# Splitting half of the W1 weights by a casting and an accumulating DMA

## The chip, the cores and the metric

The kernel runs on one core of a Trainium2 chip. A core has a matrix engine (PE, with its weight loads listed apart as PEld), a vector engine (DVE), a scalar engine (ACT), GpSimd (POOL) and SyncE (SP), and 16 DMA engines that all DMA queues share. The metric is the device time of one execution in microseconds, as the median of the runs.

## The reference

The program is a two-layer decoder trunk over 256 tokens of width 2048 in float32. Layer 0 is a gated short convolution, layer 1 latent attention with 16 heads. Each is followed by a squared-ReLU MLP of hidden width 8192, and every sublayer ends in a layer norm of `alpha*x + f(x)`. What matters here is the MLP, which runs once in each layer:

```python
def sq_relu_mlp(x, w1, w2):            # x: 256x2048, w1: 2048x8192, w2: 8192x2048
    return jnp.square(jax.nn.relu(x @ w1)) @ w2
```

## The kernel before

**Precision by two parts.** PE multiplies in a reduced float32 format (float32r). Each float32 operand is therefore split into a high part (its value rounded to float32r) and a low part (the rest, again as float32r), and a product is the sum of high by high, high by low and low by high. For a weight the split is the function `split` (lines 109 to 112): ACT writes `hi` by a copy that rounds (line 111), and DVE writes `lo = raw - hi` (line 112).

**The stream of weight units.** All weights come from DRAM in units of 128 partitions by 1024 float32 values (512 KB), in the order in which PE will use them; this order is the list `stream` (lines 64 to 83). A unit is loaded by SP into one of 5 `raw` buffers (`load_raw`, lines 130 to 133) and split into one of 8 `hi` and one of 8 `lo` buffers (`RAW, WA = 5, 8`, line 33). A `hi` or `lo` buffer is free again when PE has done the last product with the unit eight places earlier. `take` (lines 171 to 183) hands PE the next units, and before that calls `prepare` (lines 135 to 165) for units up to `LOOK = 5` places further on.

**The MLP.** It runs in 8 passes (`NQ = 8`), each over 1024 hidden columns. A pass has three stages:

- *W1 stage*: 8 chunks of 128 hidden columns. A chunk takes two units, a first half (input rows 0 to 1023) and a second half (input rows 1024 to 2047). For each of 16 blocks, `mm_run` issues a product of 512 columns with the high weights (line 190) and one of 256 columns with the low weights (line 194). The result is added up (`whole`, lines 300 to 304), passed through ReLU and square on ACT (lines 562 and 563) and split (lines 308 and 309). In pass 0, the first one of each MLP, other products are used for this stage (`mm_wide`).
- *fast stage* (in 13 of the 16 passes of the two MLPs): half of the output columns by seven products in place of eight (`down_fast`, lines 287 to 298). Each of its 4 weight pairs takes two loads and three pairs of `hi` and `lo` buffers, and some DVE work of its own (lines 142 to 165).
- *down stage*: the remaining output columns with 4 units for each block of 512 columns (`down`, lines 259 to 269), so 8 units after a fast stage.

**What sets the order.** The order of the instructions on each engine and DMA queue is fixed before the run by the scheduler of the framework, which plans with estimated times: of what it holds to be ready it puts the earlier in the program first. So an instruction may stand on its engine well ahead of work that the program names before it. At run time every engine and every queue works strictly in the planned order; what waits for a semaphore holds up all that stands behind it. POOL has almost nothing to do before the change: a few memsets, and four DMAs (line 869) at the beginning of the last stage that load the final gain and offset vectors.

Of the kernel before, what the change touches and what calls it, by code (L numbers as in the profile page):

```python
# [9 lines left out]
F32 = mybir.dt.float32  # L10
F32R = mybir.dt.float32r
AF = mybir.ActivationFunctionType
ALU = mybir.AluOpType
# [9 lines left out]
QC = FF // NQ // P  # L23
# [22 lines left out]
def trunk(ctx: ExitStack, tc: tile.TileContext, xT, vecs, w_in, w_out, w_kv, w_q, w_uk, w_uv,  # L46
          w_qn, w_qp, w_o, w1, w2, w2f, cosT, sinT, mask, ident, gb, out):
    nc = tc.nc
# [10 lines left out]
    def halves(w):  # L59

        lead = len(w.shape) - 2
        return [(w,)] if lead == 0 else [h for i in range(w.shape[0]) for h in halves(w[i])]

    stream = []
# [1 line left out]
        stream += halves(w_in[NC + m]) + halves(w_in[2 * NC + m]) + halves(w_in[m])  # L66
    stream += halves(w_out)

    def mlp_stream(l):
        out = []  # L70
        for q in range(NQ):
            out += halves(w1[l, q * QC:(q + 1) * QC])
            lead = 0
            if q in FAST[l]:
                out += [(w2f[l, q, j, 0], w2f[l, q, j, 1]) for j in range(QC // 2)]
                lead = 2
            out += halves(w2[l, q, lead:])
        return out

    stream += mlp_stream(0) + halves(w_kv) + halves(w_q)  # L80
    for g in range(4):
        stream += halves(w_uk[g]) + halves(w_qn[g]) + halves(w_uv[g]) + halves(w_qp[g])
    stream += halves(w_o) + mlp_stream(1)

    class Banks:

# [20 lines left out]
    ready = {}  # L107

    def split(hi, lo, src):

        nc.scalar.copy(hi, src)  # L111
        nc.vector.tensor_tensor(lo, src, hi.bitcast(F32), ALU.subtract)  # L112

    def tiled(w):
        return w.rearrange("p (b c) -> p b c", c=P)

    def parts(i):
        return tuple(whl.tile([P, 8, P], F32R, tag=t, name=f"{t}{i}") for t in ("hi", "lo"))
# [11 lines left out]
    def load_raw(i, src):  # L130
        raw = raws.tile([P, 1024], F32, tag="raw", name=f"raw{i}")
        nc.sync.dma_start(raw, src)
        return raw

    def prepare(i):

        if len(stream[i]) == 1:
            raw = load_raw(i, stream[i][0])
            hi, lo = ready[i] = parts(i)
            split(hi, lo, tiled(raw))  # L140
            return
        r1, r2 = (load_raw(f"{i}_{j}", src) for j, src in enumerate(stream[i]))
        out = []

        def finished(r, name):
            hi, lo = parts(name)
            split(hi, lo, tiled(r))
            out.append((hi, lo))

        b22, (b21, b12) = r1[:, BW:], (r2[:, :BW], r2[:, BW:])  # L150
        finished(r1, f"{i}_1")
        t = raws.tile([P, 1024], F32, tag="raw", name=f"raw{i}_t")
        two = "p (a c) -> p a c"
        nc.vector.tensor_tensor(t.rearrange(two, a=2), b12.unsqueeze(1).to_broadcast([P, 2, BW]),
                                r1.rearrange(two, a=2), ALU.subtract)
        finished(t, f"{i}_t")
        nc.vector.tensor_tensor(b12, b22, t[:, :BW], ALU.subtract)
        finished(r2, f"{i}_2")
        t4 = r1[:, :BW]
        nc.vector.tensor_tensor(t4, b21, b12, ALU.subtract)  # L160
        f = state["fast"].tile([P, 2, BW], F32R, tag="t4", name=f"t4_{i}")
        split(f[:, 0, :], f[:, 1, :], t4)
        b1, t13, b2 = ([[v.rearrange("p b c -> p (b c)")[:, o:o + BW] for v in w] for o in (0, BW)] for w in out)
        ready[i] = {"11": b1[0], "22": b1[1], "21": b2[0], "T2": b2[1], "T1": t13[0], "T3": t13[1],
                    "T4": [f[:, 0, :], f[:, 1, :]]}
# [5 lines left out]
    def take(halves=2):  # L171

        i = state["next"]
        state["next"] += halves
        ahead = -sum(size(j) for j in range(i, i + halves))
        for j in range(i, len(stream)):
            ahead += size(j)
            if ahead > LOOK:
                break
            if j >= state["split"]:  # L180
                prepare(j)
                state["split"] = j + 1
        return [ready.pop(i + j) for j in range(halves)]
# [295 lines left out]
    for half, cuts in enumerate(FIRST):  # L479
        pieces = [load(2 * u + half, first[:, GROUP * half + u, :], cuts) for u in range(GROUP)]  # L480
        for b0, b1 in zip(cuts, cuts[1:]):
            at = slice(8 * half + b0, 8 * half + b1)
# [502 lines left out]
```

## Time and profile before

| what | value |
|---|---|
| median of 2 runs | 2053.64 us (2053.06 to 2054.22) |
| span of the profiled execution, first to last instruction | 2049.4 us |
| PE busy | 2030.6 us (99%) |
| DVE busy | 1662.8 us (81%) |
| ACT busy | 1194.1 us (58%) |
| POOL busy | 4.5 us |
| weight loads of SP's queue | 381.04 MB, 58.7% of 16 DMA engines' time |
| mean granted clock of PE | 0.997 |

The page of the profile gives the span of the profiled execution and no total beyond it; the median of the runs is 4.2 us above that span. In the rows of groups, the columns are line, engine, operation, what is written and read, shapes and count; then, after the bar, the total busy time and the mean of one in ns; then the idle time of the engine in front of them and what ended it. Matmuls overlap each other in these rows, so their means are longer than the pace at which they follow one another.

### The profile page before, as it was taken

What the parts mean: (1) busy time and instruction counts of PE and PEld (TensorE: products, weight loads), DVE (VectorE), ACT (ScalarE), POOL (GpSimd) and SP (SyncE); (2) the same over time, 40 slices, a digit from 0 to 9 for tenths busy, and PEclk for the clock granted to TensorE, in tenths of its full rate; (3) what the DMA queues carried; (4) which work ended last, traced back from release to release, by engine and by line L of the source; (5) the groups of instructions that cost most, each with busy time, mean ns of one, the idle gap of its engine ahead of it and who ended that gap; (6) DMA issues with size and microseconds to landing.
All of it is one profiled execution on the core that took longest, in us unless ns stands there. A gap on an engine that the chain in (4) does not pass through costs nothing.

```text
span 2049.4 us, 30194 instructions
## 1 busy us (share of the span) xinstructions
PE 2030.6 (99%) x11208; PEld 1760.4 (86%) x11208; DVE 1662.8 (81%) x2602; ACT 1194.1 (58%) x1860; POOL 4.5 (0%) x25
## 2 busy tenths in 40 slices
PE   9999999999999999999999999999999999999997
PEld 8888888988888888888889998898888888888885
DVE  7667677678898988989788878776879888898988
ACT  6444445676566565655656665566656656566562
POOL 0000000000000000000000000000000000000000
PEclk9999999999999999999999999999999999999998
DMA  8666666564746557465755544656475664756653
GB/s 308 202 188 187 186 185 194 159 211 136 249 142 223 193 167 250 143 226 173 234 169 164 166 124 142 197 174 196 138 236 161 196 218 156 243 153 217 212 165 137
DMA packets 108003, 385.32 MB, mean 188 GB/s; under 512 B 11984, under 2 KB 13392, under 8 KB 107856
## 3 DMA queue, kind: packets, MB, share of 16 engines
q1 hardware_dynamic: 107136, 381.04, 58.7%
q0 software_dynamic: 576, 2.10, 0.3%
q8 instruction: 88, 1.44, 0.3%
q14 instruction: 59, 0.48, 0.1%
q10 hardware_dynamic: 144, 0.26, 0.0%
HBM read 381.25 MB, written 2.10 MB: 187 GB/s over the span
## 4 chain that ended last, share of the span: by engine, by line
PE 97%; DVE 1%; DMA 1%; issue 0%; ACT 0%; SPq 0%; DVEq 0%
PE ps_u L190 34%; PE ps_u L194 17%; PE ps_d L248 7%; PE ps_d L247 7%; PE ps_d L249 7%; PE ps_f L249 4%; PE ps_f L248 4%; PE ps_f L247 4%; PE ps_w L224 1%; PE ps_w L222 1%; PE ps_w L223 1%; PE ps_g L222 1%; PE ps_g L224 1%; PE ps_g L223 1%; PE ps_wo L190 1%; PE S L788 1%
## 5 line engine op out<-in xcount | busy, mean ns | idle before, releaser
L112 DVE TENSOR_TENSOR lo<-raw,hi 128x1024 fp32r<-128x1024 f32 x712 | 861.7, 1221 | 299.0 <-ACT hi L111 294.3
L111 ACT CAST hi<-raw 128x1024 fp32r<-128x1024 f32 x712 | 742.2, 1049 | 526.6 <-PE ps_u L190 289.5
L190 PE MATMUL ps_u<-xhl,hi 128*128 128x512 f32 x1792 | 632.2, 398 | 0.0
L194 PE MATMUL ps_u<-xhl,lo 128*128 128x256 f32 x1792 | 503.0, 281 | 0.0
L190 PEld LDWEIGHTS ps_u<-xhl,hi 128*128 128x128 f32 x1792 | 336.5, 188 | 82.3
L194 PEld LDWEIGHTS ps_u<-xhl,lo 128*128 128x128 f32 x1792 | 338.5, 189 | 0.5
L190 PE MATMUL ps_u<-xhl_a,hi 128*128 128x512 f32 x720 | 253.4, 396 | 0.0
L248 PE MATMUL ps_d<-lo,h 128*128 128x512 f32 x608 | 236.9, 390 | 0.0
L249 PE MATMUL ps_d<-hi,h 128*128 128x512 f32 x608 | 236.8, 390 | 0.0
L247 PE MATMUL ps_d<-hi,h 128*128 128x512 f32 x608 | 236.6, 389 | 0.0
L194 PE MATMUL ps_u<-xhl_a,lo 128*128 128x256 f32 x720 | 202.9, 282 | 0.0
L190 PEld LDWEIGHTS ps_u<-xhl_a,hi 128*128 128x128 f32 x720 | 135.2, 188 | 31.9
L194 PEld LDWEIGHTS ps_u<-xhl_a,lo 128*128 128x128 f32 x720 | 135.8, 189 | 0.0
L248 PEld LDWEIGHTS ps_d<-lo,h 128*128 128x128 f32 x608 | 114.1, 188 | 24.2 <-DVE lo L112 0.4
L247 PEld LDWEIGHTS ps_d<-hi,h 128*128 128x128 f32 x608 | 114.2, 188 | 24.0
L249 PEld LDWEIGHTS ps_d<-hi,h 128*128 128x128 f32 x608 | 114.1, 188 | 23.9
L111 ACT CAST hi_t<-raw_t 128x1024 fp32r<-128x1024 f32 x52 | 54.8, 1054 | 77.8 <-PE ps_u L190 41.8
L190 PE MATMUL ps_u<-z,hi 128*128 128x512 f32 x256 | 89.0, 392 | 0.0
L562 ACT ACTIVATE fh<-fh 128x256 f32<-128x256 f32 x112 | 46.4, 414 | 72.0 <-DVE fh L304 72.0
L222 PE MATMUL ps_w<-xd,hi 128*128 128x258 f32 x256 | 72.5, 284 | 0.0
L224 PE MATMUL ps_w<-xd,hi 128*128 128x258 f32 x256 | 72.5, 285 | 0.0
L223 PE MATMUL ps_w<-xd,lo 128*128 128x258 f32 x256 | 72.3, 282 | 0.0
(235 smaller groups left out, 3254.8 us busy)
## 6 DMA issues: line engine op xcount, KB each, us to landing
raw<-in_w_dram SPq DMA_DIRECT2D x408, 512.0 KB, 4.4
raw<-in_w2f_dram SPq DMA_DIRECT2D x104, 512.0 KB, 3.6
raw<-in_w_in_dram SPq DMA_DIRECT2D x90, 512.0 KB, 4.2
raw<-in_w_out_dram SPq DMA_DIRECT2D x32, 512.0 KB, 3.6
raw<-in_w_o_dram SPq DMA_DIRECT2D x32, 512.0 KB, 3.9
raw<-in_w_kv_dram SPq DMA_DIRECT2D x10, 512.0 KB, 4.3
raw<-in_w_q_dram SPq DMA_DIRECT2D x8, 512.0 KB, 4.5
raw<-in_w_uk_dram SPq DMA_DIRECT2D x8, 512.0 KB, 4.4
```

Source lines behind the costliest of these rows:

```text
L111: nc.scalar.copy(hi, src)
L112: nc.vector.tensor_tensor(lo, src, hi.bitcast(F32), ALU.subtract)
L190: nc.tensor.matmul(ps, w[blk // 8][0][:, blk % 8, :], x, start=first, stop=False)
L194: nc.tensor.matmul(ps[:, :T], w[blk // 8][1][:, blk % 8, :], x[:, :T], start=False, stop=last)
L222: nc.tensor.matmul(ps[:, :W], hi, x[k][:, :W], start=k == 0, stop=False)
L223: nc.tensor.matmul(ps[:, :W], lo, x[k][:, :W], start=False, stop=False)
L224: nc.tensor.matmul(ps[:, :W], hi, x[k][:, W:], start=False, stop=k == NC - 1)
L247: nc.tensor.matmul(ps, x[0], w[0], start=first, stop=False)
L248: nc.tensor.matmul(ps, x[0], w[1], start=False, stop=False)
L249: nc.tensor.matmul(ps, x[1], w[0], start=False, stop=last)
L562: nc.scalar.activation(f, f, AF.Relu)
L788: nc.tensor.matmul(S[:, at:at + n], qp[:, tok], kp[:, :n], start=False, stop=True)
```

## The change

The second-half units of W1 in passes 1 to 7 of each MLP, 8 in a pass and 112 in all, are no longer loaded by SP and split by ACT and DVE. For such a unit, `prepare` now issues on POOL a DMA from DRAM straight into the `hi` buffer, with a cast from float32 to float32r; then ACT writes the negated high part into the `lo` buffer; then POOL issues a second DMA of the same 512 KB from DRAM, which adds the weights onto the `lo` buffer, so that it ends as `raw - hi`. All other units are prepared as before. `mlp_stream` gets the position in the stream at which it starts, and notes which units are meant.

```diff
+    summed_lo = set()
+
-    def mlp_stream(l):
+    def mlp_stream(l, at):
         out = []
         for q in range(NQ):
+            if q > 0:
+                summed_lo.update(range(at + len(out) + 1, at + len(out) + 2 * QC, 2))
             out += halves(w1[l, q * QC:(q + 1) * QC])
...
-    stream += mlp_stream(0) + halves(w_kv) + halves(w_q)
+    stream += mlp_stream(0, len(stream))
+    stream += halves(w_kv) + halves(w_q)
...
-    stream += halves(w_o) + mlp_stream(1)
+    stream += halves(w_o)
+    stream += mlp_stream(1, len(stream))
...
     def prepare(i):
 
         if len(stream[i]) == 1:
+            if i in summed_lo:
+                hi, lo = ready[i] = parts(i)
+                nc.gpsimd.dma_start(hi, tiled(stream[i][0]))
+                nc.scalar.activation(lo, hi.bitcast(F32), AF.Copy, scale=-1.0)
+                nc.gpsimd.dma_start(lo, tiled(stream[i][0]), accum_op=ALU.add)
+                return
             raw = load_raw(i, stream[i][0])
             hi, lo = ready[i] = parts(i)
             split(hi, lo, tiled(raw))
```

## The prediction

> **What bounds the kernel now.** I read the page from the top: the busy times, the chain that ended last, then the costliest groups.
>
> ```profile
> span 2049.4 us, 30194 instructions
> ...
> PE 2030.6 (99%) x11208; PEld 1760.4 (86%) x11208; DVE 1662.8 (81%) x2602; ACT 1194.1 (58%) x1860; POOL 4.5 (0%) x25
> ...
> PE 97%; DVE 1%; DMA 1%; issue 0%; ACT 0%; SPq 0%; DVEq 0%
> ...
> L112 DVE TENSOR_TENSOR lo<-raw,hi 128x1024 fp32r<-128x1024 f32 x712 | 861.7, 1221 | 299.0 <-ACT hi L111 294.3
> L111 ACT CAST hi<-raw 128x1024 fp32r<-128x1024 f32 x712 | 742.2, 1049 | 526.6 <-PE ps_u L190 289.5 <-DMA raw<-in_w_dram 139.4 <-PE ps_d L249 38.2
> ```
>
> PE is busy 2030.6 of 2049.4 us and carries 97% of the chain. The change touches no matmul, so relief of DVE and ACT can bring back at most the 18.8 us in which PE is idle, 0.9%. The waits of PE show how little of that is theirs (who waited, for whom, us in total, times, longest):
>
> ```profile
> PE ps_g L190 <- DVE xhl_a L309: 2.1, 2, 1.4
> PE ps_f L248 <- DVE t L112: 1.4, 1, 1.4
> ...
> PEld ps_g L190 <- ACT hi L111: 2.2, 2, 1.8
> PEld ps_f L248 <- DVE t L112: 1.7, 1, 1.7
> ```
>
> These are at most 7.4 us, and the ones at `ps_g` belong to the start of the kernel. So the question is only whether the new way of making a unit is ready when PE wants it. The L111 row says that the casts wait first of all for PE (289.5 us): a `hi` buffer must come free. The lead of a unit is thus the run of eight buffers. To price it I took PE's order of time at the borders of one pass, two casts on ACT that lie one chunk apart, and busy time by stage (fast, down, W1, and a crowded window; columns PE, PEld, DVE, ACT, POOL, clock, DMA share, GB/s).
>
> ```profile
> 590.41 0.39 PE L247 MATMUL ps_f<-t,h 128*128 128x512 f32 x1
> ...
> 609.91 0.40 PE L247 MATMUL ps_d<-hi,h 128*128 128x512 f32 x1
> ...
> 631.72 0.39 PE L190 MATMUL ps_u<-xhl,hi 128*128 128x512 f32 x1
> ...
> 676.92 0.39 PE L247 MATMUL ps_f<-t,h 128*128 128x512 f32 x1
> ```
> ```profile
> 470.06 1.05 ACT L111 CAST hi<-raw 128x1024 fp32r<-128x1024 f32 x1 [0.86 <-PE ps_u L190]
> ...
> 475.72 1.05 ACT L111 CAST hi<-raw 128x1024 fp32r<-128x1024 f32 x1 [0.87 <-PE ps_u L190]
> ```
> ```profile
> 590.40:609.90 19.50, 19.50 (x86) 15.84 (x85) 17.77 (x23) 11.93 (x17) 0.00 (x0) 1.00 0.60 184
> 609.90:631.70 21.80, 21.80 (x97) 18.02 (x96) 19.63 (x23) 11.71 (x13) 0.00 (x0) 1.00 0.78 260
> 631.70:676.90 45.20, 45.20 (x257) 39.21 (x256) 38.10 (x59) 28.88 (x49) 0.00 (x0) 1.00 0.55 172
> 540.00:560.00 20.00, 20.00 (x108) 17.15 (x107) 14.44 (x16) 11.99 (x17) 0.00 (x0) 1.00 0.90 304
> ```
>
> The W1 stage is 676.92 - 631.72 = 45.2 us for 16 units, 2.82 us a unit, and the two casts confirm 5.66 us a chunk. The down stage is 631.72 - 609.91 = 21.8 us for 8 units, 2.73 us each. A buffer that comes free is wanted seven units later: **the lead** is 7 x 2.82 = 19.8 us inside the W1 stage, 7 x 2.73 = 19.1 us for units prepared in the down stage.
>
> **The change, part by part.** *Removed, hidden:* 112 subtractions of 1221 ns, 137 us of DVE's 1662.8, and 112 loads on SP's queue. DVE and SP are off the chain, so both are worth nothing by themselves; what they cover remains covered by PE. *Exchanged:* 112 casts of 1049 ns become 112 negating copies of the same shape. No row shows one with a scale on this shape; the nearest at 128x1024 is the cast, and I take 1.05 us. Even a quarter more is 30 us in all on an engine that is busy 28.9 of 45.2 us in the W1 stage. *Added:* 224 DMAs on POOL. The only rows of DMAs from POOL are the four loads of `gbt`, plain ones of the same 512 KB:
>
> ```profile
> L869 POOL DMA_DIRECT2D gbt<-in_gb_dram x4: 527/529/664, 1991.0 to 1992.7; - x4
> ...
> DMA to landing us min/median/max: 4.6/5.8/9.4
> ```
> ```profile
> q1 hardware_dynamic: 107136, 381.04, 58.7%
> ...
> raw<-in_w_dram SPq DMA_DIRECT2D x408, 512.0 KB, 4.4
> ```
>
> An issue holds POOL for 0.53 us, 119 us over the whole kernel; POOL is idle. It lands after 4.6 to 9.4 us, median 5.8, against 4.4 from SP. No trace shows a cast or an addition done by a DMA. For the cast I take 5.8 with ends 3.6 (below) and 9.4; for the accumulate 5.8 with the lower end 3.6 and the upper 18.8, twice the longest, because it must also read what it adds to. The middle of the nearest row is my value for both. The lower end is the shortest median of an SP load:
>
> ```profile
> raw<-in_w2f_dram SPq DMA_DIRECT2D x104, 512.0 KB, 3.6
> ```
>
> *The chain of one unit,* from the free buffer: cast 5.8 + half a place behind another cast on ACT 0.5 + negation 1.05 + accumulate 5.8 = 13.2 us, against a lead of 19.1: **a cover of 5.9 us** (6.6 inside the W1 stage). In before the same unit took 4.4 + 1.05 + 1.22 = 6.7 us, of which the load lay ahead of the free buffer, because the raw buffers are separate. So the change eats most of the margin, but not all of it.
>
> *Waits added.* ACT's negation waits for a DMA that starts only when PE frees the buffer; behind it on ACT wait the casts of first halves and the evacuation of finished chunks. A cast held 5.8 us is still inside its 19.8 us, and eight PSUM banks hold 8 chunks, so no PE wait follows. POOL's accumulate waits for ACT; behind it may stand the cast DMA of the next unit, and who waits for that is PE, by the rivals below.
>
> *Bandwidth.* 304 GB/s at a share of 0.90 make about 338 GB/s when full. In the down stage 260 GB/s over 21.8 us are 5.67 MB. Four of the 8 units of a pass are prepared in it, and each adds one extra 0.524 MB: 7.77 MB, 23.0 us at 338 GB/s, so 1.2 us more than the stage, inside the cover. The W1 stage needs 172 x 45.2 = 7.77 MB + 2.1 = 9.87 MB, 29.2 of 45.2 us. Over the kernel, 112 loads are 58.7 MB, 9.0 points of q1's 58.7%; twice that comes back, so the share ends near 68%.
>
> With the accumulate priced at two loads instead of one, the down stage has 9.87 MB, 29.2 us, 7.4 more than it lasts; after the cover of 5.9 that leaves about 1.5 us a pass, in 14 passes 21 us. The W1 stage still fits (12.0 MB, 35.4 us). The Trainium skill states a rule that speaks for this dearer price, in "Collectives: The Full Stack", section "The bandwidth ceiling: the fold count and why AG ≠ RS ≠ AR": a transfer that adds runs at half the rate of a copy, since it needs two source reads on the same ring. By that rule the sum would be the 21 us; no row here shows such a transfer.
>
> *Sum.* At one load's price the loss is 0, at two loads' price 21 us; I take 10 us, the middle. Span 2049.4 + 10 = 2059; the median of the runs is 4.2 us above the span: **2064 us**. Own range 2045 (all the waits above gone) to 2094.
>
> **The rivals.** *The serial loop, slower.* If the accumulate of one unit stands on POOL ahead of the cast of the next, POOL is a ring: cast 5.8, place on ACT 0.5, negation 1.05, issue 0.53 = 7.9 us per unit, while PE uses one each 5.66. It lags by 2.2 us a unit, 7 x 2.2 = 15.6 us over a pass; less the cover of 5.9, PE stands 9.7 us in each of 14 passes, 136 us: about 2190 (7.4 us a turn, without the place on ACT, gives 2140, 8.4 gives 2250). It decides from a turn of 5.66 + 5.9/7 = 6.5 us. For it: the accumulate is earlier in the program, and the casts' 139.4 us of waits for `raw` show the plan holding DMAs for quicker than they are. Against it: by the plan too a cast that needs some 4.4 us and 1.05 of ACT makes the accumulate ready at 5.5 us or later, hardly before the next buffer comes free at 5.66, and once one cast stands ahead the ring has two units in flight and the lag is gone.
>
> *Slow DMAs.* With 9.4 for the cast and 18.8 for the accumulate the chain is 29.8 us, 10 us over the lead; the buffers turn twice in a pass, so 2 x 10 x 14 = 280 us: 2330. For it: nothing shows a DMA that computes; against it: the plain ones keep 338 GB/s.
>
> *A gain.* 7.4 us at most: 2046. *Not what it says:* the set must hit the odd units; it counts from `at` plus the length so far plus 1 in steps of 2, 8 to a pass, which fits; if it hit nothing, 2054.
>
> **How the numbers follow.** Hidden or nearly so, 2064: 0.53. Serial loop, 2190: 0.27. Slow DMAs, 2330 and above: 0.17. A gain, or no effect, 2046 to 2054: 0.03. A measurement of this kernel tells about 2% from no change, 41 us, so 2094.7 is the border. The first and last case are inside it, both middle ones outside; a gain of over 2% would need more than PE's idle time: faster 0.01, same 0.55, slower 0.44. The range goes from 2045 to 2290: it holds the hidden case, the whole serial loop with its 2250, and the mild end of slow DMAs; some 0.15 are left out, nearly all above.
>
> **What would show it.** Right: PE near 2030 busy and over 97% of the chain, DVE down by about 137 us, q0 near 18% and q1 near 50%, POOL DMAs landing under 8 us, the longest PE waits for `lo` under 2 us. Serial loop: PE waiting for DMA `lo<-in_w_dram` late in W1 stages, growing from chunk to chunk and gone by the fast stage, and POOL's queue waiting for ACT with the next buffer already free. Slow DMAs: accumulates landing well over 10 us, DMA share near 1 in the W1 stage, PE waiting from the first chunk on. The prediction is wrong above all if a computing DMA has a price of its own, or if ACT, standing in front of a DMA, holds up a fast stage through its casts of `hi_t` or its copies out of PSUM.

## The result, and the profile after

The changed kernel takes 2236.97 us (median, 2231.75 to 2242.18) against 2053.64 us: a ratio of **1.0891, 95% interval 1.083 to 1.0952**. The loss is 183 us. The kernel was slower than my forecast of 2064 us by far more than that case allowed for, and it came out in the part of the range that I had kept for the rivals.

The page of the changed kernel, top to bottom (busy times; queues with packets, MB and share of 16 engines; the chain by engine; two groups; DMA issues with the median time to landing):

```profile
span 2229.9 us, 30150 instructions
...
PE 2091.7 (94%) x11208; PEld 1794.5 (80%) x11208; DVE 1539.4 (69%) x2490; ACT 1183.9 (53%) x1860; POOL 164.8 (7%) x249
...
q1 hardware_dynamic: 91008, 322.31, 45.1%
q0 software_dynamic: 32832, 119.55, 23.2%
...
PE 43%; issue 24%; DVE 14%; DMA 13%; ACT 3%; POOL 3%; DVEq 0%; POOLq 0%; ACTq 0%
...
L118 DVE TENSOR_TENSOR lo<-raw,hi 128x1024 fp32r<-128x1024 f32 x600 | 726.9, 1223 | 305.3 <-ACT hi L117 300.6
...
L147 ACT ACTIVATE lo<-hi 128x1024 fp32r<-128x1024 f32 x112 | 118.0, 1058 | 336.1 <-DMA hi<-in_w_dram 336.1
...
hi<-in_w_dram POOLq DMA_DIRECT2D x112, 512.0 KB, 6.7
lo<-in_w_dram POOLq DMA_DIRECT2D x112, 512.0 KB, 5.7
```

PE carried 97% of the chain before and carries 43% now. It is idle for 2229.9 - 2091.7 = 138.2 us, where it was idle for 18.8: 119.4 us more. The three rows of PE in the waits of the same kernel hold all of it (who waited, for whom, us in total, times, longest):

```profile
ACT lo L147 <- DMA hi<-in_w_dram: 336.1, 68, 10.7
...
DVE fh L316 <- ACT t L315: 212.3, 40, 10.8
...
POOL lo L148 <- ACT lo L147: 165.4, 34, 9.7
...
PE ps_u L206 <- DMA lo<-in_w_dram: 61.1, 30, 4.3
...
PE ps_f L259 <- ACT t L117: 31.0, 13, 3.3
PE ps_f L260 <- DVE t L118: 27.5, 13, 2.3
```

61.1 us are waits for a `lo` that the accumulating DMA has not yet finished. 31.0 + 27.5 = 58.5 us stand at the first two products of the 13 fast stages, whose pairs the change does not touch. Together 119.6. The rest of the longer span, 61.1 us, is PE's own: its busy time rose from 2030.6 to 2091.7 with the same 11208 matmuls, while the mean granted clock fell from 0.997 to 0.968 (2030.6 x 0.997 / 0.968 = 2091). Most of it is the clock, but perhaps not all: by the clock records of the two traces PE was busy for 110 us at half clock, against 3 us before, and half of the difference is about 53 us. So a third of the loss is for `lo`, a third at the fast stages, and somewhat under a third is the clock.

**Units that are late.** ACT, POOL and PE in one pass of the changed kernel (start, duration, engine, line; in brackets the idle time before it and what ended it), one fence for each engine; the last fence is the landing of the two accumulates that POOL issued at 655.24:

```profile
662.68 1.06 ACT L147 ACTIVATE lo<-hi 128x1024 fp32r<-128x1024 f32 x1 [4.44 <-DMA hi<-in_w_dram]
...
674.92 1.06 ACT L147 ACTIVATE lo<-hi 128x1024 fp32r<-128x1024 f32 x1 [10.26 <-DMA hi<-in_w_dram]
675.89 0.35 ACT L315 COPY t<-ps_u 128x256 f32<-128x256 f32 x1
```
```profile
643.85 0.55 POOL L146 DMA_DIRECT2D hi<-in_w_dram  x1 [40.98 <-PE ps_d L261]
...
655.24 1.82 POOL L148 DMA_DIRECT2D lo<-in_w_dram  x2
664.03 0.86 POOL L148 DMA_DIRECT2D lo<-in_w_dram  x1 [6.97 <-ACT lo L147]
664.56 0.89 POOL L146 DMA_DIRECT2D hi<-in_w_dram  x1
```
```profile
659.70 0.39 PE L202 MATMUL ps_u<-xhl,hi 128*128 128x512 f32 x1
...
666.86 0.58 PE L206 MATMUL ps_u<-xhl,lo 128*128 128x256 f32 x1 [3.95 <-DMA lo<-in_w_dram]
```
```profile
DMA to landing us min/median/max: 11.6/12.7/13.9
```

PE's stall is for the first of the changed units of the pass. Its cast went out at 643.85, when its buffer came free, and PE wanted its `lo` at 662.91, 19.1 us later; that is the lead of the prediction. Its accumulate was issued at 655.24, and landed only 11.6 us after that, at 666.8. The 16 DMA engines were full in this stretch (a share of 1.05 from 655.2 to 666.9 us in the table of windows).

Further on, POOL stood for 6.97 us with the accumulate of a later unit, waiting for ACT's negation of it, and with the next casting DMA behind it. The buffer of that cast came free when the down stage ended, at about 659.7. The cast went out at 664.56, half a microsecond behind the accumulate, and landed just before 674.92. ACT's next negation was planned ahead of a copy out of PSUM (line 315) that did not depend on it. ACT stood there for 10.26 us, and the copy ran only at 675.89.

**What the hold costs DVE.** Busy time of the engines in the W1 stage ahead of one fast stage. In the kernel before, the stage runs from 545.2 to 590.4 us; in the changed one the same stage runs from 560.4 to 618.9 (columns PE, PEld, DVE, ACT, POOL, clock, DMA share, GB/s):

```profile
545.20:590.40 45.20, 45.20 (x257) 39.22 (x256) 37.38 (x59) 28.55 (x49) 0.00 (x0) 1.00 0.53 166
575.20:590.40 15.20, 15.20 (x88) 13.19 (x87) 15.13 (x27) 10.38 (x19) 0.00 (x0) 1.00 0.30 81
```
```profile
560.40:580.00 19.60, 16.28 (x83) 13.81 (x83) 4.13 (x8) 5.74 (x9) 2.87 (x4) 0.91 0.91 242
580.00:600.00 20.00, 20.00 (x115) 17.36 (x114) 10.03 (x19) 10.51 (x19) 4.29 (x6) 1.00 0.85 209
600.00:618.90 18.90, 15.95 (x84) 13.05 (x82) 17.80 (x29) 14.31 (x27) 0.87 (x1) 0.99 0.55 133
```

Before, DVE idles for 7.8 us in the whole stage, and is busy for 15.13 of the last 15.2 us. Now it does 14.2 us of work in the first 39.6 us, where it mostly idles, and is then nearly full (17.80 of 18.9) while PE waits for what it has still to make. An average of 69% busy hides this.

### The profile page after: what moved, and what is told of

Its sections match the earlier page's. It is cut to its first block, busy times and chain, and to the rows that moved or that the text cites. A ratio compares the mean times of both kernels' runs of the same rounds, so it can differ in the third digit from the quotient of the medians.

```text
span 2229.9 us, 30150 instructions
## 1 busy us (share of the span) xinstructions
PE 2091.7 (94%) x11208; PEld 1794.5 (80%) x11208; DVE 1539.4 (69%) x2490; ACT 1183.9 (53%) x1860; POOL 164.8 (7%) x249
## 3 DMA queue, kind: packets, MB, share of 16 engines
q1 hardware_dynamic: 91008, 322.31, 45.1%
q0 software_dynamic: 32832, 119.55, 23.2%
## 4 chain that ended last, share of the span: by engine, by line
PE 43%; issue 24%; DVE 14%; DMA 13%; ACT 3%; POOL 3%; DVEq 0%; POOLq 0%; ACTq 0%
PE ps_u L202 15%; PE ps_u L206 8%; DMA hi<-in_w_dram 7%; DMA lo<-in_w_dram 6%; DVE lo L118 4%; PE ps_d L260 2%; PE ps_d L261 2%; PE ps_d L259 2%; POOL hi L146 2%; DVE raw_t L166 2%; DVE lo_t L118 1%; PE ps_w L236 1%; PE ps_w L234 1%; PE ps_w L235 1%; ACT lo L147 1%
## 5 line engine op out<-in xcount | busy, mean ns | idle before, releaser
L118 DVE TENSOR_TENSOR lo<-raw,hi 128x1024 fp32r<-128x1024 f32 x600 | 726.9, 1223 | 305.3 <-ACT hi L117 300.6
L117 ACT CAST hi<-raw 128x1024 fp32r<-128x1024 f32 x600 | 623.7, 1048 | 387.8 <-PE ps_u L202 199.2
L202 PE MATMUL ps_u<-xhl,hi 128*128 128x512 f32 x1792 | 652.3, 406 | 0.0
L206 PE MATMUL ps_u<-xhl,lo 128*128 128x256 f32 x1792 | 517.0, 289 | 61.4 <-DMA lo<-in_w_dram 61.1
L202 PEld LDWEIGHTS ps_u<-xhl,hi 128*128 128x128 f32 x1792 | 348.1, 194 | 82.2
L206 PEld LDWEIGHTS ps_u<-xhl,lo 128*128 128x128 f32 x1792 | 349.7, 195 | 72.7 <-DMA lo<-in_w_dram 72.2
L147 ACT ACTIVATE lo<-hi 128x1024 fp32r<-128x1024 f32 x112 | 118.0, 1058 | 336.1 <-DMA hi<-in_w_dram 336.1
L316 DVE TENSOR_TENSOR fh<-ps_u,t 128x256 f32<-128x256 f32 x112 | 47.2, 421 | 212.3 <-ACT t L315 212.3
L146 POOL DMA_DIRECT2D hi<-in_w_dram x112 | 76.9, 731 | 1226.2 <-PE ps_d L261 1029.4
L148 POOL DMA_DIRECT2D lo<-in_w_dram x112 | 98.4, 892 | 495.9 <-ACT t L315 297.7
```

The source lines that it names most:

```text
L146: nc.gpsimd.dma_start(hi, tiled(stream[i][0]))
L147: nc.scalar.activation(lo, hi.bitcast(F32), AF.Copy, scale=-1.0)
L148: nc.gpsimd.dma_start(lo, tiled(stream[i][0]), accum_op=ALU.add)
L202: nc.tensor.matmul(ps, w[blk // 8][0][:, blk % 8, :], x, start=first, stop=False)
L206: nc.tensor.matmul(ps[:, :T], w[blk // 8][1][:, blk % 8, :], x[:, :T], start=False, stop=last)
L316: nc.vector.tensor_tensor(out, ps[:, :T], t, ALU.add)
```

## The experiments

Two theories stood at the start. The *queues*: instructions stand in their planned order behind others that wait (POOL above all), whatever a byte costs. The *bytes*: a DMA that computes takes more of the DMA engines than its size says. Later a third came, the *held engine*: what ACT loses in wait for a cast, DVE lacks before a fast stage. Each run's loss is its median less the median of the kernel before on the same chip (2051.5 us for the cast alone, the accumulate alone, the forced order and the half of the units; 2052.5 for the copy in planned order, the negation on DVE and the two places in the pass; 2054.84 for the others). A loss of under 2% (41 us) rests on the interval beside it.

### Which of the two DMAs: the cast alone, the accumulate alone

`hi` by the casting DMA, and `lo` as before from a raw unit:

```diff
-                nc.scalar.activation(lo, hi.bitcast(F32), AF.Copy, scale=-1.0)
-                nc.gpsimd.dma_start(lo, tiled(stream[i][0]), accum_op=ALU.add)
+                nc.vector.tensor_tensor(lo, tiled(raw), hi.bitcast(F32), ALU.subtract)
```

> The high part by the casting DMA on POOL as in the change, but the raw weights are loaded by SP too, and DVE subtracts as before: no negation and no accumulate. Each of the 112 units is still read twice from DRAM. Theory of the queues: nothing on POOL waits for ACT, a cast needs only its free buffer, and cast 6.7 plus subtraction 1.2 us lie far inside the lead of 19 us: 2050 to 2080. Theory of the bytes: the same second read remains, only the price of the accumulate is gone: 2120 or more.

Measured: 2072.28 us, ratio 1.0096 (1.0067 to 1.0126), clock 0.996. Its casting queue:

```profile
q0 software_dynamic: 16704, 60.82, 9.2%
```

9.2% of 2070.6 us are 190.5 us of 16 engines, 3.13 us per MB; SP's plain loads take 45.1% of 2229.9 us for 322.31 MB in the changed kernel, 3.12. **A casting DMA costs what a plain one does**, and by itself it brings 21 us of the 183. The queues' number held (2050 to 2080), that of the bytes missed (2120 or more).

The reverse, `hi` by SP and ACT, then the negation and the accumulate:

```diff
-                nc.gpsimd.dma_start(hi, tiled(stream[i][0]))
+                nc.scalar.copy(hi, tiled(raw))
```

> The low part by negation and accumulating DMA as in the change, but the high part by SP's load and ACT's cast as before: no casting DMA. Each of the 112 units is still read twice, and ACT does one more pass of 1.05 us for each. Theory of the queues: ACT waits for a load that was started early, so the negation is never late, and POOL holds only accumulates: 2050 to 2090. Theory of the bytes: the accumulate, the dearer of the two DMAs, remains: 2150 to 2240.

Measured: 2173.51 us, ratio 1.059 (1.0559 to 1.062). The queues' number missed, that of the bytes held. Its queue, and a window of 10 us in which accumulates run:

```profile
q0 software_dynamic: 16704, 60.82, 14.6%
```
```profile
570.00:580.00 10.00, 10.00 (x60) 8.81 (x59) 1.96 (x4) 6.79 (x11) 1.34 (x2) 1.00 1.02 286
```

The same bytes as in the run before take 14.6% of 2170.9 us, 317 us where the casts took 190.5. And in the window the engines are full (1.02) at 286 GB/s, where the kernel before moved 304 at a share of 0.90. PE waited only 4.4 us for `lo` here, but 80 us at `ps_f` in sum: what came late were SP's loads of the fast stage's weights, for which DVE waited 86.7 us, and the work behind them.

### The order on POOL

Each accumulate is planned behind the next unit's cast, and never behind two:

```diff
+    def finish_lo(put_hi, now=None):
...
+        with behind(put_hi if put_hi is not None else own):
+            state["lo_dma"] = nc.gpsimd.dma_start(lo, tiled(stream[i][0]), accum_op=ALU.add)
...
-                nc.gpsimd.dma_start(hi, tiled(stream[i][0]))
+                with behind(state.get("lo_dma")):
+                    put_hi = nc.gpsimd.dma_start(hi, tiled(stream[i][0]))
                 nc.scalar.activation(lo, hi.bitcast(F32), AF.Copy, scale=-1.0)
-                nc.gpsimd.dma_start(lo, tiled(stream[i][0]), accum_op=ALU.add)
+                finish_lo(put_hi)
```

> All 112 units as in the changed kernel, with the same DMAs and the same negation on ACT; only POOL's order is laid down: the cast of the next unit always stands ahead of the accumulate of this one, and never two casts ahead. Theory of the queues: the ring on POOL is gone, what remains is ACT held by its negations; PE's wait for lo falls from 61 us to under 20 and the time to 2060 to 2130. Theory of the bytes: nothing changes for the DMA engines, 2220 to 2245.

Measured: 2129.09 us, ratio 1.0373 (1.0341 to 1.0405), clock 0.985. The order alone takes the loss from 183 to 78 us. By the traces it is POOL's order that differs: PE and SP work in the same order as in the changed kernel, and 6 of ACT's 1861 and 15 of DVE's 2490 instructions stand elsewhere. The time lies at the upper end of the queues' number and far from that of the bytes; the waits for `lo` are 24.1 us, not under 20. PE's waits that are left (the product of line 206 is now line 222, those of 259 and 260 are 275 and 276):

```profile
PE ps_u L222 <- DMA lo<-in_w_dram: 24.1, 13, 4.1
PE ps_f L276 <- DVE t L118: 23.3, 12, 2.3
PE ps_f L275 <- ACT t L117: 2.6, 5, 0.8
```

### Half of the units

Every second one of the units (56 in all):

```diff
-                summed_lo.update(range(at + len(out) + 1, at + len(out) + 2 * QC, 2))
+                summed_lo.update(range(at + len(out) + 1, at + len(out) + 2 * QC, 4))
```

> Only every second of the changed units is still made by the two DMAs: 4 in a pass in place of 8, 56 in all; the other 56 go back to the load by SP and the split by ACT and DVE. Theory of the queues (POOL and ACT work in a planned order, and a turn of cast, negation, accumulate and issue is longer than the 5.66 us in which PE uses a unit of this kind): the turns now come each 11.3 us, longer than a turn, so the lag cannot add up and the loss falls to under 30 us: 2054 to 2084. Theory of the bytes (the second read and the price of the computing DMAs fill the DMA engines): half of the extra bytes, half of the loss of 183 us: about 2145.

Measured: 2125.36 us, ratio 1.0355 (1.0325 to 1.0385): 74 us for half of the units. The bytes' number (about 2145) came nearer. The queues' number missed, because I had thought of POOL's ring as a lag that needs many units. POOL's row of time in this kernel shows it in one step:

```profile
627.30 0.56 POOL L146 DMA_DIRECT2D hi<-in_w_dram  x1 [47.53 <-PE ps_d L261]
638.18 0.55 POOL L146 DMA_DIRECT2D hi<-in_w_dram  x1 [10.32 <-DVE lo L118]
638.91 0.89 POOL L148 DMA_DIRECT2D lo<-in_w_dram  x1 [0.18 <-issue]
```

The first accumulate of a pass stands behind the second cast, whose buffer comes free 11 us later. So the order does harm in both directions: an accumulate can stand ahead of a cast, or behind one that cannot start yet. This run does not tell the theories apart well, since it changes the planned order too.

### The price of adding, with the order kept

The second DMA copies in place of adding, at the same place on POOL, so `lo` ends as the raw weights:

```diff
-                nc.gpsimd.dma_start(lo, tiled(stream[i][0]), accum_op=ALU.add)
+                nc.gpsimd.dma_start(lo, tiled(stream[i][0]))
```

> The second DMA of each of the 112 units stays on POOL, in the same place of the planned order and after the same negation, with the same 512 KB, but it copies instead of adding (so lo holds the raw weights and the products with the low parts are wrong in value). Theory of the accumulate's price (a DMA that adds takes 1.7 times the DMA engines' time, and what is late with it makes the stalls): 2070 to 2125, q0 at or below 20% of the 16 engines, casts landing under 6 us again, PE's waits for lo under 25 us in all. Theory of the order (instructions of POOL, ACT and DVE stand behind others that wait, whatever a byte costs): 2190 to 2240, PE's waits as they were (61 us for lo, 58 us at ps_f).

Measured: 2134.48 us, ratio 1.0391 (1.0375 to 1.0408), clock 0.984; PE's waits are 20.2 us for `lo` and 36.8 at `ps_f`. It missed the upper end for the accumulate's price by 9 us and is far from the other theory's. All engines work in the same order as in the changed kernel, so only what the second DMA does differs. The queue:

```profile
q0 software_dynamic: 32832, 119.55, 17.6%
```

17.6% of 2132.4 us are 375 us, 3.14 us per MB for all of it; in the changed kernel the same bytes took 23.2% of 2229.9, 517 us. The difference of 142 us belongs to 58.7 MB, 2.42 us per MB on top of 3.14: **adding costs 1.77 times a copy** here. The accumulate alone above gives 1.69 times, by the same reckoning. The rule of the Trainium skill that the prediction weighed ("Collectives: The Full Stack", section "The bandwidth ceiling: the fold count and why AG ≠ RS ≠ AR") is stated there for the reduce step of a collective, not for a DMA onto a buffer of the core; half the rate, 2.0 times, is somewhat dearer than what is measured here. Then both edits at once, forced order and copying:

> The forced order on POOL, and a second DMA that copies instead of adding (so lo holds the raw weights and the products with the low parts are wrong in value). If the order and the accumulate's price are two separate losses: 2055 to 2090, PE's waits for lo under 5 us and at ps_f under 15 us. If each only relieves the same hold of ACT, and that remains: 2100 to 2130, with the waits at ps_f of 20 us and more.

Measured: 2079.99 us, ratio 1.0118 (1.0085 to 1.0151), clock 0.995; 18.0 us of waits for `lo`, 4.3 at `ps_f`. The time and the waits at `ps_f` are those of two separate losses; the waits for `lo` are not (under 5 us expected). The order is that of the forced-order kernel on every engine. The four kernels make a square (loss in us):

| | second DMA adds | second DMA copies |
|---|---|---|
| order as planned | 183 | 82 |
| order forced | 78 | 25 |

Removing one of the two causes is worth 101 to 105 us with the other still there, and 53 to 57 us without it. They are two causes that share some 50 us. That the shared part is the same late units is argued, not shown.

### Who is held

The negation on DVE in place of ACT:

```diff
-                nc.scalar.activation(lo, hi.bitcast(F32), AF.Copy, scale=-1.0)
+                nc.vector.tensor_scalar(lo, hi.bitcast(F32), -1.0, None, ALU.mult)
```

> The negation moves from ACT to DVE; all else is left to the planner. If ACT's negations, standing ahead of its copies out of PSUM, are what makes the pairs of the fast stage late: PE's 31 us at ps_f for ACT t are gone, those for DVE t are at most 28, and the time is 2140 to 2200. If any engine that holds an instruction in wait for a late cast does the same: DVE is held in ACT's place, PE's waits at ps_f stay near 58 us in sum, and the time is 2200 to 2260. The theory of the accumulate's price says the second too.

Measured: 2331.28 us, ratio 1.1351 (1.1334 to 1.1368), worse than either number. PE waits 112.4 us for `lo` and 75.7 at `ps_f`; DVE itself stands for casts:

```profile
DVE lo L147 <- DMA hi<-in_w_dram: 393.0, 76, 9.7
```

It does matter which engine waits, and DVE is the wrong one. POOL's planned order differs in this kernel too, so the 279 us are not the price of the place alone. The clean form is the forced order, with POOL making the negation itself:

```diff
         with behind(put_hi if put_hi is not None else own):
+            nc.gpsimd.tensor_scalar(lo, hi.bitcast(F32), -1.0, None, ALU.mult)
             state["lo_dma"] = nc.gpsimd.dma_start(lo, tiled(stream[i][0]), accum_op=ALU.add)
...
-                nc.scalar.activation(lo, hi.bitcast(F32), AF.Copy, scale=-1.0)
```

> As in the run with the forced order on POOL (2129 us), but the negation is done by POOL itself, ahead of its accumulate, so neither ACT nor DVE stands in wait for a casting DMA. Theory of the held engine (ACT's wait keeps back its copies out of PSUM, DVE idles behind them and lacks that time before the fast stage): PE's waits at ps_f under 15 us in sum, and 2060 to 2115, the rest being waits for lo behind POOL's slower negation. Theory of the accumulate's price alone (loads and casts land late whoever waits): ps_f 20 to 45 us as with the forced order, 2115 to 2160.

Measured: 2097.8 us, ratio 1.0222 (1.0196 to 1.0248). Its waits of PE and the group of POOL's negation:

```profile
PE ps_u L222 <- DMA lo<-in_w_dram: 30.3, 35, 2.7
PE ps_f L276 <- DVE t L118: 3.4, 2, 2.0
```
```profile
L151 POOL TENSOR_SCALAR lo<-hi 128x1024 fp32r<-128x1024 f32 x112 | 334.4, 2985 | 150.8 <-DMA hi<-in_w_dram 143.4 <-PE ps_u L222 1.9 <-DVE sf L601 1.5
```

The waits at `ps_f` are gone (4.0 us in sum against 25.9 with the negation on ACT), with the accumulate as dear as ever (q0 at 24.4%) and a negation of 2.99 us in place of 1.06. PE's products and POOL's DMAs stand in the same order as with the negation on ACT; of DVE's 2490 instructions 105 stand elsewhere. So **with this order the stalls at the fast stage come from the negation on ACT**, as the held engine has it. The run took both ACT's wait and 119 us of its work away. It is not the work: with forced order and copying ACT does the same negations, and `ps_f` is down to 4.3 us as well. What is left is for `lo`: a longer chain of each unit. Nor is a held ACT the only way to a late fast stage: with the accumulate alone no engine waits for a cast, and 80 us stand at `ps_f` behind SP's late loads.

A cast that ACT waits for, with no accumulate at all (SP's raw unit is added on DVE):

```diff
+                raw = load_raw(i, stream[i][0])
...
                 nc.scalar.activation(lo, hi.bitcast(F32), AF.Copy, scale=-1.0)
-                nc.gpsimd.dma_start(lo, tiled(stream[i][0]), accum_op=ALU.add)
+                nc.vector.tensor_tensor(lo, tiled(raw), lo.bitcast(F32), ALU.add)
```

> No accumulate: hi by the casting DMA, the negation on ACT as in the change, then DVE adds a raw unit loaded by SP. DMA bytes are those of the kernel before, POOL issues only casts. Beside the run with the casting DMA alone (2072 us) it has one thing more, an ACT instruction that waits for the cast. Theory of the held engine: 2085 to 2130, with 20 to 50 us of PE's waits at ps_f. Theory of the accumulate's price: 2060 to 2080, waits at ps_f under 15 us.

Measured: 2072.32 us, ratio 1.008 (1.0061 to 1.0099). The held engine's number missed, that of the accumulate's price held (2060 to 2080, and 14.9 us at `ps_f`), and the group says why:

```profile
L148 ACT ACTIVATE lo<-hi 128x1024 fp32r<-128x1024 f32 x112 | 118.4, 1057 | 25.8 <-DMA hi<-in_w_dram 25.6
```

The instruction is the same, but POOL has nothing but casts to issue, and they land in 5.6 us (median). ACT waits 25.6 us for them in the whole kernel instead of 336.1. So standing in front of a DMA cost little where the DMA came soon. Among the runs with all 112 units and the negation on ACT behind a cast, the loss rises with ACT's wait: 25.6 us of wait and 17 us of loss here; 154.9 and 25 with forced order and copying; 219.3 and 78 with forced order; 225.8 and 82 with copying; 336.1 and 183 in the changed kernel. It is no rule of proportion, and the runs with 56 units do not fit into the row: 70.7 and 74 for every second unit, 164.6 and 94 for the late half, 203.7 and 112 for the early half.

Is DVE really short of time before a fast stage? The kernel before, with needless work for DVE and no DMA changed:

```diff
+                    for _ in range(14 if m == 5 else 0):
+                        nc.vector.tensor_tensor(sf[:, :2, :], pair[-2].rearrange("p (i c) -> p i c", i=2),
+                                                pair[-1].rearrange("p (i c) -> p i c", i=2), ALU.add)
```

> The kernel before, with no change of DMAs: DVE gets 14 needless additions of 128x256 (0.42 us each, 5.9 us) behind chunk 5 of each W1 stage that a fast stage follows, 13 times. Theory of the held engine (DVE has some 2 us to spare before a fast stage, so what it loses there PE waits for): PE's waits at ps_f 25 to 60 us, clock below 0.99, 2090 to 2140. Against it, if DVE can give 6 us there: 2050 to 2065, waits at ps_f under 10 us.

Measured: 2090.92 us, ratio 1.0177 (1.016 to 1.0194), at the lower end of the first number; the waits at `ps_f` are 9.9 us, where that number had 25 to 60. PE's waits:

```profile
PE ps_d L247 <- DVE fh L304: 14.1, 12, 1.2
PE ps_f L247 <- ACT forms L111: 9.9, 12, 1.1
PE ps_d L247 <- ACT hi L111: 4.2, 1, 4.2
```

36 us in 13 passes are 2.8 us of the 5.9 added, so an estimate of what DVE has to spare there is about 3 us, where I had named 2; the rest reaches PE. It is a rough estimate, for the planner rearranged more than I meant. In the pass from 549 us on, the additions are spread from 589 to 605 us, and the first products of the down stage stand among the last of the fast stage, which is why most of the waits are at `ps_d`. The clock did not fall (0.996), against what I wrote; the stalls are of 1.2 us and less, but for one of 4.2.

### Which place in the pass

Only the second halves of chunks 0 to 3, then only those of chunks 4 to 7:

```diff
-                summed_lo.update(range(at + len(out) + 1, at + len(out) + 2 * QC, 2))
+                summed_lo.update(range(at + len(out) + 1, at + len(out) + QC, 2))
```

> Only the second halves of chunks 0 to 3 of each pass (56 units), whose buffers come free in the down stage, where the DMA engines are 78% busy in the kernel before. Theory of the accumulate's price: these are the ones that cost, so most of the loss of all 112 is here: 2120 to 2190, with PE's waits both for lo and at ps_f. Theory of the ring on POOL (the lag grows with each unit): half the units give at most half the lag, 2060 to 2110.

```diff
-                summed_lo.update(range(at + len(out) + 1, at + len(out) + 2 * QC, 2))
+                summed_lo.update(range(at + len(out) + QC + 1, at + len(out) + 2 * QC, 2))
```

> Only the second halves of chunks 4 to 7 of each pass (56 units), whose buffers come free inside the W1 stage, where the DMA engines are 55% busy in the kernel before. Theory of the accumulate's price: the room is there, so 2054 to 2085 with PE's waits for lo under 10 us. Theory of the ring: as with the early half, 2060 to 2110, and no difference of over 15 us between the two halves.

Measured: early 2164.54 us, ratio 1.0545 (1.0527 to 1.0562); late 2146.99, ratio 1.0456 (1.044 to 1.0471). Early agrees with the bytes, with 34.3 us of waits for `lo` and 41.7 at `ps_f`. Late missed both theories. In it PE waits 2.2 us for `lo` in all, and 58.3 at `ps_f`. One pass of the late kernel, ACT, DVE and PE:

```profile
584.15 1.06 ACT L147 ACTIVATE lo<-hi 128x1024 fp32r<-128x1024 f32 x1 [5.04 <-DMA hi<-in_w_dram]
585.11 1.04 ACT L117 CAST hi_t<-raw_t 128x1024 fp32r<-128x1024 f32 x1
```
```profile
586.18 1.22 DVE L118 TENSOR_TENSOR lo_t<-raw_t,hi_t 128x1024 fp32r<-128x1024 f32 x1 [5.14 <-ACT hi_t L117]
```
```profile
602.39 0.49 PE L259 MATMUL ps_f<-t,h 128*128 128x512 f32 x1 [2.41 <-ACT t L117]
605.15 0.79 PE L260 MATMUL ps_f<-t,h 128*128 128x512 f32 x1 [2.26 <-DVE t L118]
```

ACT waits 5.04 us for a cast, with the cast of a fast pair (`hi_t`) behind it; DVE waits 5.14 us for that; 16 us later PE stands for 4.7 us. The DMA engines are 51% busy from 580 to 600 us. Neither of the two theories had this; it fits the held engine, though this run by itself shows only the order in time.

## Why the prediction was wrong, step by step

The time lies in the stated range, 2045 to 2290, but only because the range took in the serial loop beside the forecast. The forecast itself, 2064 us with its waits hidden and "same" as the likeliest outcome at 0.55, failed.

- **PE bounds the kernel, no more than 18.8 us can be won: right.** Nothing was won: no run of these edits came below the kernel before, and the nearest are the two without an accumulate (1.008 and 1.0096). The subtractions' row fell by 134.8 us (137 forecast) and DVE's total by 123.4, all off the path.
- **Negation at 1.05 us, hidden: its size right** (1.058).
- **Issue on POOL at 0.53 us: too low.** In the changed kernel an accumulate's issue holds POOL for 0.89 us and a cast's for 0.73 on average; POOL is busy 164.8 us where I had 119. That cost nothing by itself.
- **The lead of 19.1 us: right.** The unit shown above was wanted 19.1 us after its buffer came free.
- **The chain of 13.2 us and the cover of 5.9: the first step that failed.** I took 5.8 us each for the cast and the accumulate, the middle of four quiet loads. The medians are 6.7 and 5.7, but of the units shown above a cast took 10.3 us and two accumulates 11.6 and 13.9, on full engines. The accumulate of 11.6 us ended a chain of 23.0 us. A cover of 5.9 us is spent by the slow units, not by the median one, and by POOL's order: 6.97 us of standing in one place.
- **The accumulate between one and two loads: right, at 1.7 to 1.8.** What I made of it failed. I asked whether each stage's bytes fit into its time, and got 21 us at two loads' price; with the order as it was, the price was worth 101 us, and 53 with the order forced. The step sums bytes over a stage and says nothing of the DMAs that queue in the full part of it: the casts, and SP's loads for the fast stage.
- **"Eight PSUM banks hold 8 chunks, so no PE wait follows": wrong.** I followed ACT's held copies only to PSUM, and not to DVE, which waited for them 40 times (212.3 us) and has by the estimate above some 3 us to spare before a fast stage. 58.5 us of PE's waits are there; with the order forced they were 25.9, and with the negation taken off ACT as well 4.0.
- **The serial loop, 2190: the nearest case, half of its mechanism.** POOL did wait for ACT with a cast behind it, and undoing the order brought back 105 us. But it did not build up over 7 units; the planned order is mixed, single places of 7 to 11 us do it, and of PE's 119.6 us of waits only 61.1 are for `lo`. That the result lies in its 2140 to 2250 is partly luck: its 136 us had no clock and no fast stage in them. The upper end is also added up too high: a turn of 8.4 us gives (8.4 - 5.66) x 7 - 5.9 = 13.3 us a pass, 186 in all, and 2240.
- **Slow DMAs, 2330: not so.** Medians of 6.7 and 5.7 us, far from 9.4 and 18.8.
- **The clock was in no step.** PE's busy time grew by 61 us, about 53 of them lost to half clock, on top of the 119.4 us of stalls.
- **The signs.** Of those for the hidden case, q0 came at 23.2% instead of near 18, PE at 43% of the chain instead of over 97, and the longest wait for `lo` at 4.3 us instead of under 2. Both reasons in the last sentence came true, the DMA's own price and ACT holding up the fast stage; I had named them and given the second no number.

Still open: the 17 to 21 us of the casting DMA alone, which stand partly at `ps_f` (11.7 us and 14.9) and are not traced to a place; and how the 43 us with POOL's negation divide between that slower instruction and the accumulate. A negation planned later on ACT was not tried.

## What to carry to other kernels

Before an instruction is set to wait for a DMA, look up what stands behind it on its engine, and who waits for that, down to the engine that has the least time to spare in the next stage; a busy share over the whole kernel does not show that engine, a table of windows does. Two DMAs that depend on each other through another engine need their order on the issuing queue written out, and a lead reckoned with the slowest landing in the full stretch, not the median. A stall of a bound PE can cost more than its length: here 119 us of added stalls, most of it in stalls of 2 us and more, came with some 53 us lost to the clock.

## What the runs showed of the hardware

**Adding in a DMA costs 1.7 to 1.8 times the engine time of a copy; casting costs nothing extra.** 5.56 us of 16 engines per MB against 3.14 for a copy and 3.13 for a cast, from the queues above. With the order forced the same pair of runs gives 1.73 times, and the accumulate alone 1.69.

**The clock can halve after a stall of under 3 us.** The start of a fast stage in the changed kernel, PE's row of time and then windows (the clock is the sixth column):

```profile
618.88 0.80 PE L259 MATMUL ps_f<-t,h 128*128 128x512 f32 x1 [2.81 <-ACT t L117]
621.64 0.80 PE L260 MATMUL ps_f<-t,h 128*128 128x512 f32 x1 [1.96 <-DVE t L118]
```
```profile
618.80:619.40 0.60, 0.52 (x1) 0.29 (x1) 0.57 (x1) 0.60 (x2) 0.00 (x0) 0.50 0.09 34
...
622.00:625.00 3.00, 3.00 (x8) 2.33 (x8) 3.00 (x6) 1.61 (x4) 0.00 (x0) 0.50 0.71 242
...
628.00:631.00 3.00, 3.00 (x15) 2.42 (x14) 3.00 (x4) 2.85 (x4) 0.00 (x0) 1.00 0.37 90
```

The clock is at half before the second stall begins, so the first, of 2.81 us, was enough. PE stays at half clock until about 625: 8 matmuls in 3 us, where 15 go at full clock. In the run with the forced order a lone stall of 2.25 us did the same, from 696.35 to 698.60:

```profile
699.00:702.00 3.00, 3.00 (x9) 2.35 (x8) 3.00 (x6) 1.57 (x4) 0.00 (x0) 0.50 0.67 217
```

The Trainium skill, "TensorE: Matmul & The Clock Gate", section "What's actually happening", states half clock after an idle window of about 3.4 us; these stalls were shorter. The runs give no length from which it happens. In the run with the negation on POOL, 35 stalls of 0.87 us on average and 2.7 at most left the mean clock at 0.997, as in the kernel before. PE's busy time rose by 14.9 us even there, against 61.1 in the changed kernel.
